# Last mLSTM head scanned alongside its projection, first output weights fetched inside the scan, and one weight pool and three product banks kept open behind it

## Chip, cores and metric

One core of one Trainium2 chip runs the whole program once. The metric is the device time of one execution in microseconds. The core has five engines: TensorE (PE, with its weight loads as PEld), VectorE (DVE), ScalarE (ACT), GpSimd (POOL) and SyncE (SP), which issues most of the transfers. TensorE writes its products into PSUM, eight banks of 128 x 512 float32; the other engines carry them on.

## What is computed

One layer of a diffusion backbone over 1152 rows (128 of context, block 0, and 1024 of latent tokens, blocks 1 to 8), width 1024. Two head groups run side by side, then one output projection merges them and a SwiGLU FFN follows:

```python
aq, ak, av, mq, mk, mv, mo, mg = split(h @ w_in)
attn_o = attention(aq, keys, vals)
hm, st_f, st_b = mlstm_bidir(...)          # 4 heads, chunks of 128, forward and backward
hm = rmsnorm(hm) * sigmoid(mo)
mix = concat([attn_o, hm]) @ w_out
x = x + g1 * mix
x = x + g2 * swiglu(rmsnorm(x) * (1 + sc2) + sh2)
```

A chunk b of an mLSTM head and one direction needs the state C at its edge: `num = (q k^T * D) v + inter * (q C)`, and `C_next = decay * C + k^T (w * v)`. The forward state goes from block 1 to 8, the backward state from 8 to 1.

## The kernel before

Float32 products are made from parts: an operand is split into a rounded high part and the rest (`whi`/`wlo`, `th`/`tl`), and three products (high x high, high x low, low x high) are summed in one bank. `load_piece` (L141) loads 512 KB of a weight into a `raw` tile, ScalarE casts it to the high part (L157), and VectorE subtracts to get the low part (`sub`, L137).

The order of the work on each engine is not written out by hand. The program is traced as generators that are woven at given rates, `hot(n)` raises the priority of what it encloses, `tc.issue_after` orders an instruction behind another of the same engine, and a planner that simulates the engines with estimated times makes each engine's fixed order from that. The engines then wait for one another at run time only.

The stages around the change:

- `head_project(h)` (L774) projects one mLSTM head: first the queries of three groups of 384 rows, then keys, values and output gate of the nine blocks, 0 to 8. After each block `evac` copies the results, transposes the keys (`kT`, L797 to L799), and `update` (L811) makes the block's k^T(wv) for both directions. The forward state is linked at once on VectorE (L824); the backward addend is copied by ScalarE (L828) and kept in `raws`.
- `head_mlstm(h)` (L857) scans one head. It begins with seven backward links on VectorE (L862). For each block, `weights(b)` makes q k^T and the decay matrix in one product bank (L875 to L878), ScalarE takes the exponential (`dt`, L881), VectorE multiplies (`sd`, L883). Then come the products with the two states (L898, scaled into `it`, L901), with the values (L905), their sum (`nu`, L908), the division, the gate and the rmsnorm (`rsqrt`, L121 to L134, twelve small VectorE operations), a GpSimd multiplication (L928) and the store to `hm_d` (L931, L933). The scan of head h is woven into the projection of head h + 1. The last head's scan stands alone: three blocks' `weights` are made ahead, the scan's own products use the two `wi` banks, and the norm is made for three blocks at a time.
- Beside that last scan run `attn_out_first` (L1281: the attention half of the output projection for blocks 0 to 2, both halves n of the columns, with `out_block`, L1179) and the last part of the adaLN modulation (`ada_rest`, strip products L364). They borrow tiles: weights in the `iraw` and `ipair` tiles, gates in `gta`, operands in `mxa`.
- Then the pools are closed: `hTp`, `gp`, `mlp` and the weight pool `wpi`, and the two PSUM pools `wi` (2 banks) and `mm` (3 banks). New ones are opened on the same memory: four `mm` banks, one `po` bank, a weight pool of 4 pairs and 2 `raw` tiles, and a pool `wl` with a fifth pair. A tile in a new pool waits for the tiles that lay at its place.
- `prefill` (L1188) makes the mLSTM half of the output projection for nine blocks: it loads rows of `hm_d` (L1198, L1200), transposes them (`mix`, L116), splits them (L1227, L137), multiplies with two pieces of `w_out` for each half (L1183 to L1185), adds gated to x (L1144, L1145), and for blocks 0 to 2 makes the second norm. Attention of the second group of blocks is woven in. After that the FFN fills TensorE to the end (L1389 to L1391, L1155 to L1157).

## Time and profile before

| | us |
|---|---|
| median of three runs | 1533.34 (1533.31 to 1536.2) |
| the profiled execution | 1535.49 |
| its span, first to last instruction | 1533.7 |
| TensorE busy | 1475.5 |
| VectorE busy | 1019.8 |
| ScalarE busy | 772.3 |
| GpSimd busy | 266.7 |

The span is what the trace covers; the execution lasts 1.8 us longer. All times in traces count from the first instruction. An arrow names what ended a wait. Consecutive matmuls overlap, so the time from one start to the next is what one costs, and not its own duration. The granted clock is the share of TensorE's full clock, 1.00 where nothing is held back.

### The profile page before, as it was taken

The page shows a single profiled execution, that of the slowest core. Times are in us where ns is not written, and L with a number is a line of the kernel's source. Part 1 is how long each engine was busy: PE and PEld are TensorE (multiplying, and loading weights), DVE is VectorE, ACT ScalarE, POOL GpSimd, SP SyncE. Part 2 cuts the span into 40 slices and gives each one's busy share as a digit, 9 for nine tenths or more (in the row PEclk, how much of TensorE's full clock was granted, in tenths as well). Part 3 has the DMA queues.
Part 4 walks back from the last instruction along what each step waited for, and adds up shares of the span by engine and source line. Part 5 has one row for each costly group of instructions (what it writes and reads, how often), then busy time and mean ns, then how long its engine had stood idle before and what let it go on. Part 6 is the DMA issues. An engine that isn't in the chain of part 4 may idle for free.

```text
span 1533.7 us, 23404 instructions
## 1 busy us (share of the span) xinstructions
PE 1475.5 (96%) x8539; PEld 1242.4 (81%) x8539; DVE 1019.8 (66%) x2025; ACT 772.3 (50%) x1429; POOL 266.7 (17%) x354
## 2 busy tenths in 40 slices
PE   6799999999988899999999999999999999999997
PEld 3545567677766689999898989989898989999996
DVE  4887655838657875877646587887856584554454
ACT  4765475847644554555333445656553443323333
POOL 0213423333434341010010101001010101101110
PEclk9899999999999999999999999999999999999999
DMA  9664323524365666979645457977854454544441
GB/s 362 193 204 156 92 70 42 119 52 72 79 207 166 161 161 179 214 167 193 165 119 156 138 169 230 190 175 171 187 134 145 139 163 154 158 134 137 140 145 56
DMA packets 387113, 233.77 MB, mean 152 GB/s; under 512 B 170102, under 2 KB 347462, under 8 KB 386998
## 3 DMA queue, kind: packets, MB, share of 16 engines
q1 hardware_dynamic: 385006, 228.69, 54.7%
q10 hardware_dynamic: 1864, 3.20, 1.1%
q8 instruction: 67, 1.10, 0.3%
q14 instruction: 48, 0.39, 0.1%
q0 software_dynamic: 128, 0.39, 0.1%
HBM read 182.21 MB, written 11.69 MB: 126 GB/s over the span
## 4 chain that ended last, share of the span: by engine, by line
PE 61%; DVE 3%; ACT 1%; issue 0%; DVEq 0%
PE mm L1390 12%; PE mm L1391 12%; PE mm L1389 12%; PE mm L1155 5%; PE mm L1156 5%; PE mm L1157 5%; PE S L1075 3%; PE po L1099 2%; PE po L1100 2%; PE mm L1183 1%; PE mm L1185 1%; PE mm L1184 1%; DVE fl L1378 1%; DVE wlo L137 1%; DVE t L1144 0%; DVE x L1145 0%
## 5 line engine op out<-in xcount | busy, mean ns | idle before, releaser
L157 ACT CAST whi<-raw 128x1024 fp32r<-128x1024 f32 (+1 forms) x216 | 221.8, 1027 | 386.8 <-PE mm L1390 143.9
L137 DVE TENSOR_TENSOR wlo<-raw,whi 128x1024 fp32r<-128x1024 f32 (+1 forms) x216 | 260.4, 1206 | 182.4 <-ACT whi L157 180.8
L1390 PE MATMUL mm<-aTl,whi 128*128 128x384 f32 x1056 | 355.9, 337 | 2.7 <-DVE aTl L137 2.7
L1391 PE MATMUL mm<-aTh,wlo 128*128 128x384 f32 x1056 | 354.3, 336 | 0.0
L1389 PE MATMUL mm<-aTh,whi 128*128 128x384 f32 x1056 | 353.1, 335 | 0.0
L137 POOL TENSOR_TENSOR hl<-tn,hl 128x384 fp32r<-128x384 f32 x66 | 83.8, 1270 | 847.4 <-ACT hl L1412 755.5
L1390 PEld LDWEIGHTS mm<-aTl,whi 128*128 128x128 f32 x1056 | 198.4, 188 | 3.9 <-DVE aTl L137 3.3
L1389 PEld LDWEIGHTS mm<-aTh,whi 128*128 128x128 f32 x1056 | 198.1, 188 | 0.5
L1391 PEld LDWEIGHTS mm<-aTh,wlo 128*128 128x128 f32 x1056 | 198.4, 188 | 0.1
L1156 PE MATMUL mm<-wlo,hl 128*128 128x512 f32 x372 | 145.5, 391 | 0.0
L1155 PE MATMUL mm<-whi,hl 128*128 128x512 f32 x372 | 144.2, 392 | 0.0
L1157 PE MATMUL mm<-whi,hl 128*128 128x512 f32 x372 | 142.8, 392 | 0.0
L1082 DVE SCALAR_TENSOR_TENSOR pl<-pr,st,ph 128x1152 f16<-128x1152 f32 (+1 forms) x72 | 96.3, 1337 | 36.6 <-ACT ph L1081 36.5
L1078 ACT ACTIVATE pr<-S,st 128x1152 f32<-128x1152 f32 (+1 forms) x72 | 81.3, 1129 | 38.4 <-DVE st L1077 36.6
L1077 DVE TENSOR_REDUCE st<-S 128x1 f32<-128x1152 f32 (+1 forms) x72 | 88.8, 1233 | 11.9 <-PE S L1075 11.3
L1081 ACT ACTIVATE ph<-pr,st 128x1152 f16<-128x1152 f32 (+1 forms) x72 | 83.8, 1164 | 22.7 <-DVE st L1080 9.9
L506 PE MATMUL wi<-headw,hT 128*128 128x384 f16 x288 | 93.9, 326 | 0.2 <-ACT th L792 0.2
L508 PE MATMUL wi<-headw,hT 128*128 128x384 f16 x288 | 93.9, 326 | 0.0
L507 PE MATMUL wi<-headw,hT 128*128 128x384 f16 x288 | 93.9, 326 | 0.0
L1075 PE MATMUL S<-kst,qT 128*128 128x384 f32 (+1 forms) x400 | 84.9, 344 | 4.0 <-ACT pr L1078 3.9
L1144 DVE TENSOR_TENSOR t<-mm,gl 128x512 f32<-128x512 f32 x102 | 68.7, 684 | 24.7 <-DMA gl<-g_d 9.3
L1157 PEld LDWEIGHTS mm<-whi,hl 128*128 128x128 f32 x372 | 69.9, 188 | 14.4
(396 smaller groups left out, 2639.8 us busy)
## 6 DMA issues: line engine op xcount, KB each, us to landing
raw<-in_w_gu_dram SPq DMA_DIRECT2D x132, 512.0 KB
raw<-in_w_down_dram SPq DMA_DIRECT2D x60, 512.0 KB
a<-in_w_ada_dram SPq DMA_DIRECT2D x24, 512.0 KB
gl<-g_d SPq DMA_DIRECT2D x36, 256.0 KB
aw<-in_w_ada_dram SPq DMA_DIRECT2D x16, 512.0 KB
iraw<-in_w_in_dram SPq DMA_DIRECT2D x32, 256.0 KB
raw<-in_w_out_dram SPq DMA_DIRECT2D x12, 512.0 KB
x<-in_x_sample_dram SPq DMA_DIRECT2D x11, 512.0 KB
```

The lines of the kernel that those rows point to most:

```text
L137: (dve if eng == "dve" else pool).tensor_tensor(out=out, in0=full, in1=hi, op=ALU.subtract)
L157: nc.scalar.copy(hi[:, :n], raw[:, :n])
L506: mm(ps[:, :n], ah, wh[:, k % 2, c0 : c0 + n], start=(k == 0), stop=False)
L507: mm(ps[:, :n], ah, wl[:, k % 2, c0 : c0 + n], start=False, stop=False)
L1075: mm(S[:, n, 0:w], qT[:, h, :], kst[kv][:, t, c0 + n * w : c0 + (n + 1) * w], start=(t == 0), stop=(t == 1))
L1082: dve.scalar_tensor_tensor(out=plv, in0=prv, scalar=st[:, 3:4], in1=phv, op0=ALU.mult, op1=ALU.subtract)
L1155: mm(ps, ah, wh[:, k % 2, :], start=(k == 0), stop=False)
L1156: mm(ps, ah, wl[:, k % 2, :], start=False, stop=False)
L1157: mm(ps, al, wh[:, k % 2, :], start=False, stop=(k == nk - 1))
L1389: mm(ps, wh[:, k, :], th[:, k, :], start=(k == 0), stop=False)
L1390: mm(ps, wh[:, k, :], tl[:, k, :], start=False, stop=False)
L1391: mm(ps, wl[:, k, :], th[:, k, :], start=False, stop=(k == KD - 1))
```

## The change

- **The last head's projection and scan.** Its blocks are projected in the order 0, 8, 7, ..., 1, and the backward state, not the forward one, is linked as they come. The forward links (seven) are issued in the scan, one for each block, by `link(0, b)`. The scan's generator is started inside the projection of the last block, so that `weights(0)` is issued there.
- **The end of head 2's scan.** Its rsqrt, multiplication and stores become a function `tail`, which is issued behind the `sd` of block 2 of the last scan. The weight pieces of `attn_out_first` are ordered behind `dt` and `sd` of that block too. The copy of the keys of block 1 has a raised priority.
- **First output weights.** A function `ahead` loads rows 0 and 1 of `hm_d` into the place of a query tile and the first two pieces of `w_out` of the prefill, one after the other, through a part of `gta`, before the old pools are closed.
- **Pools.** The weight pool stays open to the end. Its tiles carry new tags in twos, and five pairs are used in turn, two of them in new pools (`wq`, `wl`). The `mm` pool stays open with its three banks; a pool `mm1` adds one bank, which every fourth request of `bank()` takes. Queries of a head are one tile, not three.
- **`out_block`.** Four products with the weights' high parts, four with their low parts, and four with the input's low part come one after the other; before, the three stood together for each k.

The diff, cut to its core:

```diff
+DOWNWARD = [(0,)] + [(b,) for b in range(NB - 1, 0, -1)]
-    es_wp = ExitStack()
-    wp = es_wp.enter_context(tc.tile_pool(name="wpi", bufs=1, reuse_waits="tile"))
+    wp = ctx.enter_context(tc.tile_pool(name="wpi", bufs=1, reuse_waits="tile"))
+    turn_of = [0]
     def bank():
-        return psum["mm"].tile([P, 512], F32, name=nm("mm"), tag="mm")
+        turn_of[0] += 1
+        at = psum["mm"] if "mm1" not in psum or turn_of[0] % 4 else psum["mm1"]
+        return at.tile([P, 512], F32, name=nm("mm"), tag="mm")
...
-        raw = raw or wp.tile([P, 1024], F32, name=nm("raw"), tag="raw", bufs=2)
+        raw = wp.tile([P, 1024], F32, name=nm("raw"), tag="iraw1", bufs=2) if raw is None else raw
...
-            at, bufs = (wp, 4) if loaded["n"] else (wl, 1)
-            own = [at.tile([P, 1024], F32R, name=nm(t), tag=t, bufs=bufs) for t in ("whi", "wlo")]
+            tag = ("wl", "ipair1", "ipair0", "iraw0", "wq")[loaded["n"]]
+            at = homes.get(tag, wp)
+            own = [at.tile([P, 1024], F32R, name=nm(t), tag=tag, bufs=2) for t in ("whi", "wlo")]
...
     def head_project(h, st):
+        along = 1 if h == NH - 1 else 0
...
-            st["act"] = nc.scalar.copy(kT, pt[:, 0:P])
+            with hot(300 if b == 1 and along else 0):
+                st["act"] = nc.scalar.copy(kT, pt[:, 0:P])
...
-                if d == 0 and b > 0:
-                    st["dve"] = dve.scalar_tensor_tensor(out=cn, in0=states[0, b], scalar=decb[:, b * 4 + h : b * 4 + h + 1], in1=add,
+                if d == along and b > 0:
+                    col = d * 64 + b * 4 + h
+                    st["dve"] = dve.scalar_tensor_tensor(out=cn, in0=states[d, b], scalar=decb[:, col : col + 1], in1=add,
                                              op0=ALU.mult, op1=ALU.add)
-                    states[0, b + 1] = cn
+                    states[d, b + 1 - 2 * d] = cn
...
-        for i, _ in enumerate(linear_tok(pieces, P, 3 * P, evac, SINGLES)):
+        for i, _ in enumerate(linear_tok(pieces, P, 3 * P, evac, DOWNWARD if along else SINGLES)):
...
+            if along and i == (NB - 1) * KD:
+                next(st["scan"])
...
     def head_mlstm(h, st):
+        def link(d, b):
+            col = d * 64 + b * 4 + h
+            dve.scalar_tensor_tensor(out=st["raw"][b], in0=states[d, b], scalar=decb[:, col : col + 1], in1=st["raw"][b],
+                                     op0=ALU.mult, op1=ALU.add)
+            states[d, b + 1 - 2 * d] = st["raw"][b]
+        alone = h == NH - 1
+        if not alone:
+            for b in range(NBL, 1, -1):
+                link(1, b)
...
-        ahead = [weights(b) for b in range(depth)]
+        ahead = []
+        if alone:
+            ahead.append(weights(0))
+            yield
+        ahead += [weights(b) for b in range(len(ahead), depth)]
+        while alone and tails:
+            with behind("sd"):
+                tails.pop()()
         yield
         for b in range(NB):
+            if alone and 1 <= b < NBL:
+                link(0, b)
...
     def out_block(ws, n, th, tl):
         for k in range(4):
-            wh, wl = ws[n][k // 2]
+            wh = ws[n][k // 2][0]
             mm(ps, th[:, k], wh[:, k % 2, :], start=(k == 0), stop=False)
-            mm(ps, th[:, k], wl[:, k % 2, :], start=False, stop=False)
-            loaded["pe"] = mm(ps, tl[:, k], wh[:, k % 2, :], start=False, stop=(k == 3)).ins
+        for k in range(4):
+            mm(ps, th[:, k], ws[n][k // 2][1][:, k % 2, :], start=False, stop=False)
+        for k in range(4):
+            loaded["pe"] = mm(ps, tl[:, k], ws[n][k // 2][0][:, k % 2, :], start=False, stop=(k == 3)).ins
...
-        hms = [load_hm(0), load_hm(1)]
-        ws = [out_pieces(1, 0)]
+        hms = hms_first
+        ws = [ws_first]
...
-                    with tc.issue_after(sts[-1]["act"].ins), tc.issue_after(sts[-1]["dve"].ins):
+                    with tc.issue_after(sts[-1]["act"].ins), tc.issue_after(sts[-1]["dve"].ins), behind("dt"), behind("sd"):
...
+        spare = gt[:, 0:2].rearrange("p a b -> p (a b)")
+        def ahead():
+            rows = mlp.tile([P, NCH * CT], F32, name="hmra", tag="qTm", bufs=2)
+            hms = [rows[:, b * 512 : (b + 1) * 512] for b in range(2)]
+            for b in range(2):
+                dma(hms[b], hm_d[0][b * P : (b + 1) * P, :])
+            return out_pieces(1, 0, spare), hms
...
     emit(scan)
+    ws_first, hms_first = ahead()
     es1.close()
-    es_wp.close()
     es_d.close()
-    for name, bufs in (("mm", 4), ("po", 1)):
+    for name, bufs in (("mm1", 1), ("po", 1)):
...
-    wp = ctx.enter_context(tc.tile_pool(name="wp", bufs=1, reuse_waits="tile"))
+    homes["wq"] = ctx.enter_context(tc.tile_pool(name="wq", bufs=1, reuse_waits="tile"))
-    wl = ctx.enter_context(tc.tile_pool(name="wl", bufs=1, reuse_waits="tile"))
+    homes["wl"] = ctx.enter_context(tc.tile_pool(name="wl", bufs=1, reuse_waits="tile"))
```

68 lines of the change are left out of this document (37 added, 31 removed).

## The prediction

> **What bounds the kernel now.** I read the page's busy shares first, then the busy time by stage, then TensorE's waits inside the stages that are not full, and last the single instructions around those waits.
>
> ```profile
> span 1533.7 us, 23404 instructions
> ...
> PE 1475.5 (96%) x8539; PEld 1242.4 (81%) x8539; DVE 1019.8 (66%) x2025; ACT 772.3 (50%) x1429; POOL 266.7 (17%) x354
> ```
>
> TensorE is busy 1475.5 of 1533.7 us, so it bounds the kernel, and an edit that leaves its work alone can win at most what it idles or runs at a low clock. The table of stages says where that is (columns: width, then busy us of PE, PEld, DVE, ACT, POOL, then the granted clock, DMA share, GB/s).
>
> ```profile
> 0.00:140.00 140.00, 114.32 (x770) 64.44 (x770) 104.53 (x364) 84.12 (x175) 21.38 (x25) 0.95 0.72 241
> 437.00:442.00 5.00, 4.68 (x38) 3.83 (x35) 2.73 (x10) 2.80 (x11) 1.42 (x5) 1.00 0.96 353
> 442.00:448.00 6.00, 3.20 (x23) 2.38 (x22) 5.68 (x15) 5.34 (x14) 2.65 (x4) 1.00 0.54 200
> 448.00:455.00 7.00, 6.19 (x32) 4.11 (x32) 5.91 (x18) 1.53 (x6) 2.62 (x2) 0.51 0.69 224
> 455.00:482.00 27.00, 27.00 (x173) 19.98 (x172) 17.35 (x47) 11.29 (x35) 11.27 (x12) 1.00 0.35 112
> 482.00:493.00 11.00, 7.49 (x38) 4.67 (x37) 10.56 (x39) 7.44 (x22) 5.62 (x7) 1.00 0.87 282
> 493.00:502.00 9.00, 8.04 (x36) 6.04 (x37) 6.71 (x18) 3.16 (x4) 1.70 (x4) 1.00 0.73 234
> 502.00:510.00 8.00, 6.29 (x33) 5.17 (x32) 5.71 (x8) 3.63 (x5) 4.37 (x4) 1.00 1.00 326
> 510.00:519.00 9.00, 5.86 (x29) 4.85 (x28) 8.49 (x25) 4.49 (x9) 4.32 (x3) 1.00 0.61 145
> 519.00:524.00 5.00, 4.80 (x19) 3.96 (x18) 4.69 (x14) 5.00 (x9) 0.00 (x0) 0.66 0.31 57
> 560.00:1500.00 940.00, 937.19 (x5146) 868.27 (x5145) 622.24 (x885) 422.74 (x553) 86.69 (x68) 1.00 0.61 163
> ```
>
> The start (0 to 140) is not touched, and from 560 on 937.19 of 940 us are busy. The scan of the last head begins at 442, the prefill of the output projection at about 487; between 442 and 524 TensorE idles 2.80 + 0.81 + 3.51 + 0.96 + 1.71 + 3.14 + 0.20 = 13.1 us (width less busy time). Twice the clock falls as well: 0.51 over 448 to 455, of which 6.19 us were busy, loses 6.19 x 0.49 = 3.0 us of work; 0.66 over 519 to 524 loses 4.80 x 0.34 = 1.6. So **17.7 us** is all there is to win here.
>
> ```profile
> PE S L1075 <- ACT pr L1078: 3.1, 1, 3.1
> PE mm L875 <- DVE sd L883: 2.1, 1, 2.1
> PE mm L1184 <- DVE wlo L137: 1.9, 4, 0.6
> PE mm L1185 <- DVE mx L137: 1.7, 1, 1.7
> PE mm L1183 <- ACT mx L1227: 1.1, 1, 1.1
> PE wi L905 <- DVE nu L908: 0.8, 2, 0.4
> PE mm L364 <- DVE sd L883: 0.8, 1, 0.8
> PE mm L875 <- ACT kT L799: 0.6, 1, 0.6
> ```
>
> These eight waits, all between 437 and 524, are 12.1 us of it, and VectorE is behind most of them.
>
> **The change part by part.** It adds and removes no matmul, no decay link, no weight cast and no transfer; it moves them. So I cost positions and take TensorE's work as constant.
>
> *Start of the last scan.* Now, seven backward links (L862), the whole rsqrt of the previous head and two weight subtractions stand on VectorE before or between the first `sd` (L883), and the three product banks stay held until `sd` has read them.
>
> ```profile
> 446.85 0.49 PE L875 MATMUL mm<-qT,kT 128*128 128x128 f32 x2 [2.13 <-DVE sd L883]
> ```
> ```profile
> 446.38 0.41 DVE L883 TENSOR_TENSOR sd<-mm,dt 128x256 f32<-128x256 f32 x1
> ...
> 451.13 2.09 DVE L862 SCALAR_TENSOR_TENSOR cs<-cs,decb,cs 128x129 f32<-128x129 f32 x1
> ...
> 489.01 1.23 DVE L137 TENSOR_TENSOR wlo<-raw,whi 128x1024 fp32r<-128x1024 f32 x1
> ```
> ```profile
> L862 DVE SCALAR_TENSOR_TENSOR cs<-cs,decb,cs 128x129 f32<-128x129 f32 x6 | 3.8, 634 | 0.0
> ```
>
> Afterwards weights(0) with its `sd` lies in the projection of block 1 (where TensorE is full: 4.68 of 5.00), the seven links (3.8 us for six of them) go to the blocks of the scan, forward ones now, since the backward ones take the forward ones' place in the projection, and the subtractions and the rsqrt are queued behind the third `sd`. At 442 `sd`(0) is there; weights(1), weights(2), one pair of L905 and the first strip products then fill TensorE while ScalarE and VectorE make `sd`(1) and `sd`(2). What is late next is block 1's keys (kT, 0.6 us now) and the first `dt`/`sd` pair. Of the 2.80 + 0.81 = 3.61 us idle I keep 1.2 (0.6 for kT, as much for `sd`): gain **2.4**, bounds 0 and 3.6. Queued behind the waiting subtractions on VectorE are only the first product's operands; their cover is the scan itself, and without it one subtraction costs 1.23.
>
> *The clock.* The dip starts right after these gaps. With 1.2 us idle I expect none, because 482 to 493 idles 3.51 in 11 us and keeps 1.00: gain **3.0**, bounds 0 and 3.0. By the Trainium skill ("TensorE: Matmul & The Clock Gate", The HAM clock gate) one idle window of about 3.4 us halves the clock and one busy window restores it. The trace agrees with the half; by that rule a dip that stays would cost an estimated 1.7 and leave this term 1.3.
>
> *End of the scan and the first output weights.*
>
> ```profile
> 476.66 0.37 SPq L931 DMA_DIRECT2D hm_d<-hm  x1
> 480.84 0.82 SPq L1198 DMA_DIRECT2D hmr<-hm_d  x2
> 481.75 0.90 SPq L156 DMA_DIRECT2D raw<-in_w_out_dram  x2
> ```
> ```profile
> 487.24 1.09 PE L116 MATMUL mm<-ident,hmr 128*128 128x128 f32 x8 [0.59 <-DVE nu L908]
> 489.42 0.50 PE L1183 MATMUL mm<-whi,mx 128*128 128x512 f32 x1 [1.09 <-ACT mx L1227]
> ```
> ```profile
> 466.56 0.69 DVE L1322 TENSOR_TENSOR gta<-mm,gta 128x512 f32<-128x512 f32 x1 [0.58 <-PE mm L1185]
> ```
>
> Now the rows of h and the weights are asked for only at 480.84 and 481.75, and the transposes wait for a scan bank (`nu`). Afterwards four transfers move ahead on SP: two rows of h and two weight pieces of 512 KB. The first piece needs the gates of half 0, last read at 466.56 + 0.69 = 467.3; the second needs the same staging tile after the first's subtraction. From issue to the end of its subtraction a piece takes 8.5 us now (481.75 to 489.01 + 1.23), so they would be ready by about 476 and 484, or 4 earlier with the earlier scan: the weights leave the path. What is late next is the h rows: the store at 476.66 waits for block 2's scaling, and its landing for the load; on SP nothing urgent stands behind them but the next strip's weights, whose cover is the scan. If block 2 comes some 4 us earlier, the h rows land before the scan ends, the transposes take a product bank instead of a scan bank, and their chain (2.2 us from 487.24 to 489.42) runs under the last scan blocks. Of 3.51 I keep 1.0 (the two `nu` waits and a rest): gain **2.5**, bounds 0 and 3.5. The 0.96 of 493 to 502 are two waits for a low part whose piece was loaded late; its staging tiles are now free when the first half ends: gain **0.9**, bounds 0 and 1.0.
>
> *Lower parts last.*
>
> ```profile
> 508.98 0.39 PE L1183 MATMUL mm<-whi,mx 128*128 128x512 f32 x1
> 509.21 0.40 PE L1184 MATMUL mm<-wlo,mx 128*128 128x512 f32 x1
> ```
>
> The same twelve matmuls; the first use of the input's low part moves from third to ninth place. At 0.23 us from start to start that is 6 x 0.23 = 1.4 us more for VectorE, out of the 1.71 idle in 502 to 510: gain **1.4**, bounds 0 and 1.7. The weight load per matmul is unchanged (8539 of each).
>
> *Banks.* Four interchangeable banks become three and one that every fourth request must take. I put it at nothing because the FFN is full, and keep the other end below.
>
> *Links beside GpSimd.* The link of 2.09 us ran beside this instruction and ended with it, against 0.34 for the others ((3.8 - 2.09) / 5).
>
> ```profile
> 450.84 2.23 POOL L928 TENSOR_TENSOR hm<-hm,ry 128x1152 f32<-128x1152 f32 x1 [4.67 <-DVE dn L915]
> ```
>
> GpSimd is busy 11.27 of 27 us in the scan (42%). Seven links moved there, each held up to 1.75 longer, cost VectorE 7 x 0.42 x 1.75 = 5.1 at most, with 27 - 17.35 = 9.65 us free; each link is issued a block before its state is read. I charge **1.2** between 0 and 5.1, nearer the free time. The Trainium skill ("SBUF — State Buffer", Who interferes with whom) says that a VectorE instruction with two SBUF inputs and a GpSimd one reading SBUF lock each other out for a whole instruction. The trace agrees (2.09 beside 2.23), and the rule speaks against this part of the change.
>
> *Left alone.* The 3.14 at 510 to 519 (S waits for the softmax's exponential) and the 1.6 of clock after it: VectorE is busy 8.49 of 9 there with other work; I take 0, between a loss of 3 and a gain of 4.7.
>
> **Sum:** 2.4 + 3.0 + 2.5 + 0.9 + 1.4 - 1.2 = 9.0 us. The profiled execution took 1535.49 us (span 1533.7 and 1.8 around it), which would become 1526.5; it stands 2.15 above the median of the runs, 1533.34, from which I count: 1533.34 - 9.0 = **1524.3**.
>
> **The rivals.** *Links in the way:* the 5.1 falls on TensorE in full instead of 1.2: 1524.3 + 3.9 = **1528.2**. For it speaks the 2.09; against it, the block of lead. *Nothing gained:* the planner issues the early loads and links where they stood, or the gap only moves from `sd` to the h rows; the time stays at about **1533**. For it: order here is a plan by estimated times, not by these. *The fourth bank (slower):* requests of raised priority, six of attention and eighteen of the second norm, take the turn of a bank whose holder is issued later, and TensorE waits one evacuation each.
>
> ```profile
> L1144 DVE TENSOR_TENSOR t<-mm,gl 128x512 f32<-128x512 f32 x102 | 68.7, 684 | 24.7 <-DMA gl<-g_d 9.3
> ```
>
> 24 x 0.684 = 16.4 us against a gain of 9.0: **1540.7**, deciding from 9.0 / 24 = 0.38 us each. Against it: 5146 matmuls in 937 us are 0.18 each, a product of 24 takes 4.4 us, and a bank comes round only after three others. *More:* the stall at 514 and its clock go too: 1524.3 - 4.7 = **1519.6**.
>
> **How the numbers follow.** Forecast 0.54 (its own range 1520.5 to 1528), links 0.14, nothing gained 0.13, the fourth bank 0.13, more 0.06. A measurement of this kernel tells about 0.2% (3.1 us) from no change, so faster means below 1530.3 and slower above 1536.4: faster 0.72 (forecast, more, nearly all of links), same 0.15, slower 0.13. The range is 1517 to 1534: below it 0.03, above it the bank and some of "nothing gained", 0.16.
>
> **What would show it.** Right: TensorE at least 85% busy in the first 6 us after the projection, clock 1.00 there, no wait on `wlo`, `mx` low or `nu` over 0.5, output matmuls beginning about 7 us earlier. Wrong: a clock of 0.5 after the projection, waits of L898 on a link, or waits on banks spread through the FFN. The forecast fails if the plan around the attention of the second group changes for the worse by over 3 us.

## The result and the profile after

In ten runs of each, the kernel after took 1531.24 us (median, 1527.66 to 1535.33) and the kernel before 1535.99 (1533.31 to 1538.19). The ratio is 0.9971, 95% interval 0.9962 to 0.9979: **4.5 us faster** (0.0029 x 1536; the medians differ by 4.75), where 9.0 were forecast. The predicted 1524.3 lies 6.9 below the measured time; 2.65 of that is the base, since before's median was 1533.34 in the three runs I counted from. The direction was right and the size was not. The time lies in the range, but the prediction's own line for "faster", 1530.3, was drawn from the lower base: by it 1531.24 would have counted as the same, while the ratio is clear of 1. The profiled execution of the kernel after took 1531.07 us.

From the page of the kernel after:

```profile
span 1529.3 us, 23410 instructions
...
PE 1473.0 (96%) x8539; PEld 1244.7 (81%) x8539; DVE 1015.8 (66%) x2025; ACT 770.4 (50%) x1429; POOL 268.8 (18%) x354
```

TensorE's busy time is 2.5 us less (1475.5 before), yet its idle time fell only from 58.2 to 56.3 us (span less busy). The idle time was mostly moved, not removed. The table by stage (columns as in the prediction) shows where to:

```profile
442.00:448.00 6.00, 4.29 (x37) 3.76 (x35) 4.60 (x14) 4.94 (x17) 2.74 (x4) 1.00 0.01 3
448.00:455.00 7.00, 5.89 (x51) 4.14 (x52) 6.97 (x31) 4.80 (x16) 0.46 (x1) 1.00 0.70 225
455.00:482.00 27.00, 24.21 (x149) 17.48 (x148) 21.38 (x60) 12.49 (x36) 13.78 (x14) 1.00 0.59 188
482.00:493.00 11.00, 9.11 (x51) 6.80 (x50) 9.27 (x19) 5.34 (x12) 5.03 (x4) 1.00 0.84 257
493.00:502.00 9.00, 7.39 (x36) 6.08 (x36) 5.87 (x19) 3.51 (x9) 1.88 (x3) 1.00 0.58 189
502.00:510.00 8.00, 8.00 (x40) 6.78 (x39) 7.51 (x11) 3.39 (x5) 7.15 (x4) 1.00 1.07 268
510.00:519.00 9.00, 7.06 (x35) 5.48 (x34) 8.68 (x34) 6.72 (x12) 3.84 (x3) 0.95 0.64 137
519.00:524.00 5.00, 4.42 (x12) 3.28 (x11) 3.58 (x17) 4.61 (x9) 0.79 (x1) 0.50 0.38 99
...
560.00:1500.00 940.00, 936.74 (x5141) 870.62 (x5140) 620.69 (x881) 420.12 (x552) 88.63 (x68) 1.00 0.61 162
```

Read width less PE busy. The first two rows idle 1.71 + 1.11 = 2.8 us (before 3.6) and the clock is 1.00 where it was 0.51. But 455 to 482, full before, now idles 2.8. The next four rows idle 1.9, 1.6, 0.0 and 1.9 (before 3.5, 1.0, 1.7, 3.1). The clock at 519 to 524 still falls, to 0.50. From 560 on nothing changed (936.74, before 937.19). The waits of TensorE between 430 and 560 name the new idle time (us in total, times, longest):

```profile
PE mm L120 <- ACT y L1414: 1.8, 1, 1.8
PE mm L1219 <- ACT mx L1265: 1.8, 1, 1.8
PE mm L370 <- DVE sd L903: 1.8, 1, 1.8
PE mm L1219 <- DVE mx L141: 1.6, 1, 1.6
PE mm L370 <- DMA ip<-in_w_ada_dram: 1.5, 2, 0.8
PE mm L479 <- ACT hmx L470: 0.9, 1, 0.9
PE mm L1221 <- DVE ir L141: 0.7, 1, 0.7
PE wi L936 <- DVE nu L939: 0.6, 2, 0.4
```

The waits on S, on `kT` and on `wlo` are gone; the one on `sd` is 1.8 instead of 2.1 + 0.8. The two on `mx` stay (1.8 + 1.6, before 1.1 + 1.7); the 1.6 now stands before a block's first product (L1219), which reads the high part. The wait on `y` (in the second norm) is new, and so are those on `hmx`, `ir` and `ip`, in the middle of the scan.

Of the signs that the prediction named, the clock of 1.00 after the projection came. TensorE was busy 4.29 of the first 6 us there (71%, where 85% were named), a wait of 1.6 ended with the subtraction for `mx` (at most 0.5 was named), and the output matmuls began only 0.8 us earlier than before (489.42), not 7:

```profile
488.60 1.19 PE L1219 MATMUL mm<-whi,mx 128*128 128x512 f32 x4 [1.81 <-ACT mx L1265]
```

None of its signs of being wrong showed either: what went wrong is not among them.

**The two executions by work done.** To see gains and losses by stage I weighed each matmul with the usual start-to-start distance of its shape in the trace (the 35th percentile) and read, for a time of before, when the other execution had done the same sum. The table has the change of that offset in us in each stretch (minus is a gain). All rows are against the one profiled execution of before; the first column, in which the work of all kernels is the same, is chance of the execution (−0.4 to +3.1). Runs of one kernel spread over some 3 to 10 us, so whether a kernel is faster is read from the ratios below, and only the place of a gain from this table.

| kernel | to 150 | 150–442 | 442–454 (start of scan) | 454–478 (middle) | 478–544 (end, prefill) | 544 to end | sum |
|---|---|---|---|---|---|---|---|
| after | 0.6 | 0.8 | −4.6 | +4.1 | −5.5 | 0.3 | −4.4 |
| after again (a0) | 0.6 | 0.4 | −4.6 | +5.2 | −5.7 | −1.0 | −5.1 |
| before, other bank split (e8) | 1.7 | 0.6 | −1.4 | −0.2 | −2.5 | 0.2 | −1.7 |
| before, new order of products (e11) | 0.0 | 0.3 | −1.6 | 0.6 | 0.2 | 1.0 | 0.5 |
| after, start of scan undone (e10) | 0.8 | 1.7 | −4.0 | +6.2 | −2.5 | −0.9 | 1.3 |
| after, links in one piece (e4) | 1.2 | 0.2 | −4.6 | +3.8 | −5.6 | −1.0 | −6.1 |
| after, links spread (e5) | 2.0 | 0.3 | −5.5 | +4.7 | −5.6 | 2.0 | −1.9 |
| after, no early rows and weights (e6) | 1.2 | 0.4 | −3.8 | +3.2 | −3.4 | −1.6 | −4.1 |
| after, old order of products (e7) | 2.4 | 0.1 | −4.6 | +4.0 | −3.5 | −0.2 | −1.8 |
| after, both of these (e14) | 1.5 | 0.4 | −4.6 | +2.4 | −3.1 | 0.9 | −2.6 |
| after, tail in its old place (e1) | 1.6 | 0.5 | −3.2 | +1.1 | −3.9 | −1.9 | −5.7 |
| after, two tiles exchanged (e2) | 3.1 | 0.4 | −4.6 | +2.1 | −4.2 | 0.8 | −2.5 |
| after, weights not behind the third `sd` (e12) | 0.5 | 2.4 | −2.3 | +3.1 | −7.1 | 0.9 | −2.6 |
| after, banks in other order (e3) | 1.3 | −0.4 | −4.6 | +4.4 | −7.5 | 0.5 | −6.2 |
| after, e2 and e3 together (e9) | −0.4 | −1.0 | −4.6 | +3.6 | −4.2 | 0.0 | −6.6 |
| e9, strip's weights first (e13) | −0.2 | −1.0 | −4.6 | +1.5 | −4.1 | −1.8 | −10.2 |

So the theory to test: the start of the scan and its end gained about what was forecast, the middle gave 4 back because the moved transfers and subtractions now stand in its way, and the order of the banks cost 1. Rivals: the links are the cause at one of these places; the early loads or the order of products are the whole gain; the fourth bank costs.

### The profile page after: what moved, and what is told of

Same layout as the page of the kernel before. It is cut to its first block, busy times and chain, and to the rows that moved or that the text cites. A ratio compares the mean times of both kernels' runs of the same rounds, so it can differ in the third digit from the quotient of the medians.

```text
span 1529.3 us, 23410 instructions
## 1 busy us (share of the span) xinstructions
PE 1473.0 (96%) x8539; PEld 1244.7 (81%) x8539; DVE 1015.8 (66%) x2025; ACT 770.4 (50%) x1429; POOL 268.8 (18%) x354
## 4 chain that ended last, share of the span: by engine, by line
PE 78%; DVE 5%; DMA 3%; ACT 3%; issue 1%; POOL 1%; SPq 0%; ACTq 0%; DVEq 0%; POOLq 0%
PE mm L1437 11%; PE mm L1436 11%; PE mm L1435 11%; PE mm L1191 5%; PE mm L1192 5%; PE mm L1193 5%; PE S L1111 4%; PE wi L514 3%; PE wi L513 3%; PE wi L512 3%; PE mm L1219 2%; PE po L1136 2%; PE po L1135 2%; PE mm L1221 2%; PE mm L1223 2%
## 5 line engine op out<-in xcount | busy, mean ns | idle before, releaser
L163 ACT CAST whi<-raw 128x1024 fp32r<-128x1024 f32 x214 | 219.2, 1026 | 367.8 <-PE mm L1436 146.9
L141 DVE TENSOR_TENSOR wlo<-raw,whi 128x1024 fp32r<-128x1024 f32 x214 | 257.7, 1204 | 170.5 <-ACT whi L163 167.0
```

The costliest lines, as they stand in the source:

```text
L141: (dve if eng == "dve" else pool).tensor_tensor(out=out, in0=full, in1=hi, op=ALU.subtract)
L163: nc.scalar.copy(hi[:, :n], raw[:, :n])
```

## The experiments

Every kernel was timed in five rounds, with 5 to 12 runs of each. The ratios are against the kernel before in the same group of runs; its medians in the four groups, each on another chip, were 1535.59, 1535.84, 1535.49 and 1535.97.

### The same kernel again: a0_after

No edit. Expected:

> The changed kernel again, unaltered, as the mark for the runs beside it. Its lead over the kernel before should be 4 to 5 us again (ratio 0.9971). If the lead moves by over 2 us, single differences of 1 us between the other kernels say nothing.

Measured: 1531.92 us, ratio 0.9969 [0.9956, 0.9982]. The gain repeats.

### Do the links matter? e4_links_first and e5_links_late

The prediction had the links spread over the scan. The trace of the kernel after shows that they are not (VectorE, start and duration):

```profile
444.86 0.35 DVE L878 SCALAR_TENSOR_TENSOR cs<-c,decb,cs 128x129 f32<-128x129 f32 x1
...
447.60 0.41 DVE L903 TENSOR_TENSOR sd<-mm,dt 128x256 f32<-128x256 f32 x1
...
450.05 0.36 DVE L878 SCALAR_TENSOR_TENSOR cs<-cs,decb,cs 128x129 f32<-128x129 f32 x1
```

The first and the last of the seven are shown: all run within 5.6 us at the start, around the second `sd`. e4 issues them there in one piece:

```diff
+        if alone:
+            for b in range(1, NBL):
+                link(0, b)
...
-            if alone and 1 <= b < NBL:
-                link(0, b)
```

> The changed kernel with the seven forward links issued together at the start of the last scan, where the backward ones stood before. Theory of the prediction (the links' place clogs VectorE and so costs the clock): TensorE idles over 3 us in the first 8 us after the projection, the clock falls to 0.5, and the kernel is 4 to 5 us slower than the changed one. Rival (in the changed kernel the links ran between 444.9 and 450.4 anyway, and what kept the clock is weights(0) being ready with its sd inside the projection): within 1.5 us of the changed kernel, clock 1.00 after the projection.

Measured: 1530.14 us, 0.9963 [0.9948, 0.9978], as the rival has it; the clock stays up:

```profile
448.00:455.00 7.00, 6.44 (x53) 4.62 (x54) 6.97 (x31) 4.81 (x16) 0.46 (x1) 1.00 0.74 222
```

e5 really spreads them, each behind the `sd` of the next block:

```diff
-            if alone and 1 <= b < NBL:
-                link(0, b)
...
+            if alone and 1 <= b < NBL:
+                with tc.issue_after(st["sd", min(b + 1, NB - 1)]):
+                    link(0, b)
```

> The kernel after with each forward link tied behind the sd of the block after it, so that the seven links really are spread over the scan; in the kernel after they ran in one row at its start (444.9 to 450.4) beside the second and third sd. Theory (the links at the start are why 1.8 us of the wait on sd stay): that wait shrinks by about 1 us, ratio 0.9965. Rival (sd waits for the chain from product over exponentials to VectorE, links or no links): the wait stays at 1.5 to 2, the time within 0.7 us of the kernel after, ratio 0.997.

Measured: 1534.61 us, 0.9990 [0.9980, 1.0001], slower than the kernel after. Three of TensorE's waits between 430 and 560, in the same columns:

```profile
PE wi L931 <- ACT it L934: 1.7, 1, 1.7
...
PE wi L931 <- DVE cs L878: 1.1, 1, 1.1
PE mm L370 <- DVE sd L903: 0.7, 1, 0.7
```

The wait on `sd` fell to 0.7 as the theory has it, so the links are 1 us of it. But that won nothing: the strip's matmul behind it began at 448.09, against 448.06 in the kernel after, and a scan block then waited 1.1 for a state (`cs`) and another 1.7. The rest of the lost time stands after 544 (+2.0 in that stretch: TensorE waited 2.63 us at 581 for the attention's transposed exponentials). No cause for that one is shown. What follows: the place of the links explains neither the gain nor its missing half.

### Is the early start the gain? e10_no_early

```diff
-            if along and i == (NB - 1) * KD:
-                next(st["scan"])
```

> The kernel after, but the last scan isn't begun inside the last head's projection: its first weights (product, exponentials, sd) are issued at the end of the projection with the second and third, as before. The other parts stay. Theory (this part took the first clock dip away, since the place of the links did not): sd(0) comes back to about 446, TensorE idles over 3.5 us between 442 and 455, the granted clock falls to about 0.5 there again, and 2 to 4 us of the gain go: ratio about 0.999. Rival (the dip went because the rsqrt and the store of the head before were put off, or because of a small change of phase): clock 1.00 at 442 to 455, within 1 us of the kernel after, ratio 0.997.

Measured: 1537.31 us, 1.0010 [0.9998, 1.0022]. The size was more than the theory gave: without the early `weights(0)` nothing is left of the gain, 0.0039 x 1536 = 6.0 us. But its mechanism was wrong. The clock by stage:

```profile
448.00:455.00 7.00, 6.44 (x50) 5.21 (x51) 6.67 (x27) 4.03 (x11) 0.00 (x0) 1.00 0.46 146
455.00:482.00 27.00, 22.30 (x146) 15.84 (x145) 22.06 (x61) 12.27 (x38) 12.14 (x12) 0.94 0.56 187
...
493.00:502.00 9.00, 7.22 (x26) 5.84 (x27) 5.50 (x14) 4.19 (x12) 0.52 (x2) 0.63 0.79 240
```

At 448 to 455 it is 1.00; the idle time of 442 to 455 is 1.81 + 0.56 = 2.4, less than in the kernel after, and the start of the scan gains 4.0 of the 4.6. So the early `weights(0)` is not what keeps the clock up there. The loss comes later: 4.7 us idle in the 27, and a clock of 0.63 at 493. One gap makes most of it, here on TensorE:

```profile
465.69 1.23 PE L934 MATMUL wi<-va,sd 128*128 128x129 f32 x4 [3.69 <-DVE nu L937]
```

and on VectorE, whose `nu` it waits for:

```profile
458.64 2.06 DVE L944 TENSOR_TENSOR dn<-dn,QT 128x2 f32<-128x2 f32 x1
...
464.04 1.25 DVE L135 TENSOR_TENSOR rt<-ry 128x3 f32<-128x3 f32 x1
465.22 0.41 DVE L937 TENSOR_TENSOR nu<-wi,it 128x258 f32<-128x258 f32 x1
```

with GpSimd beside them:

```profile
458.56 2.12 POOL L958 TENSOR_TENSOR hm<-hm,ry 128x1152 f32<-128x1152 f32 x1 [0.93 <-DVE ry L137]
...
464.02 1.26 POOL L1359 TENSOR_TENSOR x1a<-x1a,gta 128x512 f32<-128x512 f32 x1 [1.34 <-DVE ry L137]
```

The usual time of that `dn` (L944) is in its own view, min, median and max in ns:

```profile
L944 DVE TENSOR_TENSOR dn<-dn,QT x36: 142/163/2057, 224.6 to 496.8; 128x2 f32<-128x2 f32 x36
```

Its 163 ns became 2057. It ended with GpSimd's scaling of the nine blocks of head 2 (458.56 + 2.12 = 460.68, 458.64 + 2.06 = 460.70); an `rt` took 1.25 beside GpSimd's 1.26. The first stands in the chain from numerator to output, the second straight ahead of `nu`. My reading, which no run separates: without the early start the put-off closing work of head 2 meets the scan where it has no lead. A kernel with neither the early start nor the put-off work, but with the rest of the change, was not run.

### Early loads and the order of products: e6_no_ahead, e7_old_k, e14_start_alone, e11_new_k

e6 loads rows and first weights where they were loaded before:

```diff
-        hms = hms_first
-        ws = [ws_first]
+        hms = [load_hm(0), load_hm(1)]
+        ws = [out_pieces(1, 0)]
...
-    ws_first, hms_first = ahead()
```

> The changed kernel with the first two rows of h and the first two output weight pieces asked for in the prefill again, as before the change. Theory (the early fetch is worth 3 us at the end of the scan): waits of the output matmuls on wlo or on the rows of h come back between 482 and 500, together 2 to 4 us, and the kernel is 2 to 4 us slower than the changed one. Rival (what starts the prefill is the gates tile gta and the rows of h, which are no earlier): within 1 us.

e7 takes the products of `out_block` back into their old order:

```diff
-            wh = ws[n][k // 2][0]
+            wh, wl = ws[n][k // 2]
             mm(ps, th[:, k], wh[:, k % 2, :], start=(k == 0), stop=False)
-        for k in range(4):
-            mm(ps, th[:, k], ws[n][k // 2][1][:, k % 2, :], start=False, stop=False)
-        for k in range(4):
-            loaded["pe"] = mm(ps, tl[:, k], ws[n][k // 2][0][:, k % 2, :], start=False, stop=(k == 3)).ins
+            mm(ps, th[:, k], wl[:, k % 2, :], start=False, stop=False)
+            loaded["pe"] = mm(ps, tl[:, k], wh[:, k % 2, :], start=False, stop=(k == 3)).ins
```

> The changed kernel with the three products of each k side by side again in the output blocks. Theory (a late low part is hidden by eight matmuls instead of two): 1 to 2 us slower than the changed kernel, with waits on wlo or on the low part of mx of 0.3 to 1.7 us each in the prefill. Rival (the first high part is late as well, so that the order does not matter): within 0.7 us.

e14 is both edits, which leaves the start of the scan, what is put off behind it, and the pools:

> The kernel after with the interleaved order of the output matmuls and without the early h rows and first weights, so that only the early start of the last scan, what is put off behind it, and the banks and pools are left of the change. Theory (the parts pay only together: the start hands 4.6 us to the middle of the scan, which gives 4 of them back unless the later waits are gone as well): ratio 0.9985 to 1.000. Rival (the start is the whole gain and the other parts are worth nothing): ratio as in the kernel after, 0.997.

e11 is the kernel before with the same lines the other way round, so with the new `out_block` alone:

> The kernel before with one part of the change alone: the twelve matmuls of an output block go through all high parts first, then the weights' low parts, then the input's low parts. Theory (undoing it cost 2 to 3 us, so it is worth as much alone): the waits on the input's low part (1.7) and half of those on wlo (1.9) go, TensorE idles 2 to 3 us less between 493 and 519, ratio about 0.9985. Rival (it is worth something only where the first output weights come early, as in the changed kernel): the wait turns to wlo and the time stays within 1 us of before, ratio 0.9995 to 1.0005.

Measured: e6 1531.48 us, 0.9972 [0.9962, 0.9983]; e7 1534.03, 0.9989 [0.9979, 0.9999]; e14 1533.02, 0.9978 [0.9968, 0.9988]; e11 1537.32, 1.0011 [1.0001, 1.0021]. In e6 the rows of h do come late, and TensorE waits for them:

```profile
PE mm L120 <- DMA hmr<-hm_d: 2.7, 1, 2.7
```

Yet the time is that of the kernel after: what the early rows save is spent on the first input tile (`mx` 1.8 at 488.60) and in the middle of the scan (3.8 to 5.2 lost with them in after, a0, e4 and e7, 3.2 and 2.4 without, in e6 and e14). The new order of products made the kernel before no faster, if anything slower (e11: the wait on S was 4.1 there). Undoing it in the kernel after cost 0.0018 x 1536 = 2.8 us, more than its theory's 1 to 2, with intervals that touch, but undoing it together with the early loads cost only 0.0007 x 1536 = 1.1, with intervals that overlap. So I read both parts together as **about 1 us, not surely above nothing**, where the prediction had 4.8, and leave open how they divide. The two traces say where it went: both parts gain 2.4 at the end (5.5 against e14's 3.1), and the middle loses 1.7 more with them (4.1 against 2.4). e14 lies between its two expectations, about as far from one as from the other; by its median the early start, what is put off behind it and the pools are 0.0022 x 1536 = 3.4 us, most of the gain.

### What the middle gave back: e1_tail_back, e2_swap_homes, e12_no_behind

In the kernel after, `hmx`, the strip's rows, lies in a tile that still holds head 2's output, whose put-off store is issued late. On ScalarE:

```profile
463.62 0.58 ACT L470 COPY hmx<-mm 128x512 f32<-128x512 f32 x1 [2.00 <-DMA hm_d<-hm]
```

and on SyncE, which issues the transfers:

```profile
457.87 0.37 SPq L963 DMA_DIRECT2D hm_d<-hm  x1
...
463.60 0.27 SPq L477 DMA_DIRECT2D hmx<-in_b_ada_dram  x1
...
466.10 1.02 SPq L1369 DMA_DIRECT2D hmra<-hm_d  x2
...
469.74 0.93 SPq L451 DMA_DIRECT2D ip<-in_w_ada_dram  x2
```

The store goes at 457.87 (453.10 before); ScalarE's copy into `hmx` waits 2.00 for it, and SyncE stands until 463.60. The strip's last weights (L451) are asked for at 469.74, behind the early rows (L1369), though the kernel is ahead of before, which asked at 468.42. e1 puts the closing work of head 2 back:

```diff
-                if h != NH - 2:
-                    tails.pop()()
+                tails.pop()()
```

> The kernel after, but the closing part of head 2 (rsqrt, scaling, store) is issued at the end of head 2's scan again, not behind the third sd of the last scan. Theory (the put-off store holds the strip rows hmx, and that is about half of what the middle of the scan gave back): the wait on hmx (0.9) and ScalarE's 2.0 behind the store go, TensorE idles under 2 of the 27 us in 455 to 482 instead of 2.8, and the clock at 442 to 455 stays 1.00; the kernel is 0 to 2 us faster than the one after, ratio 0.996 to 0.997. Rival (the put-off is what keeps the start of the scan free): the wait on sd at 448 grows from 1.8 to over 2.5, the clock there falls below 0.9, and the kernel is 2 us slower, ratio 0.9985.

e2 exchanges `hmx` with the early rows' tile:

```diff
-        hmx = mlp.tile([P, NB, P], F32, name="hmx", tag="hm", bufs=2).rearrange("p b n -> p (b n)")
+        hmx = mlp.tile([P, NCH * CT], F32, name="hmx", tag="qTm", bufs=2)
...
-            rows = mlp.tile([P, NCH * CT], F32, name="hmra", tag="qTm", bufs=2)
+            rows = mlp.tile([P, NB, P], F32, name="hmra", tag="hm", bufs=2).rearrange("p b n -> p (b n)")
```

> The kernel after with two tiles exchanged: the strip rows hmx lie where the early h rows (hmra) lay and the other way round, so that hmx no longer waits for the put-off store of head 2. Theory (that store holds hmx, which costs the mid-scan 0.9 to 2 us): the wait of 0.9 on hmx at 464 and ScalarE's 2.0 on the store go, TensorE's idle time in 455 to 482 falls from 2.8 to under 1.9, and the time falls by 1 to 2 us: ratio about 0.996. Rival (another wait stands right behind it): idle time of 455 to 502 together as in the kernel after (6.3 us), the time within 0.7 us of it, ratio 0.997.

e12 drops the order that keeps the strip's output weights behind the third `sd`:

```diff
-                    with tc.issue_after(sts[-1]["act"].ins), tc.issue_after(sts[-1]["dve"].ins), behind("dt"), behind("sd"):
+                    with tc.issue_after(sts[-1]["act"].ins), tc.issue_after(sts[-1]["dve"].ins):
```

> The kernel after without the order that puts the strip's first output weights (load, cast, subtraction) behind the third block's exponentials and sd; the load now goes as early as its staging tile allows, as before. Theory (that order delays the low parts ir, so it is the other half of what the middle of the scan gave back): the waits on ir (0.7) and on the next strip weights (0.8) shrink, idle time in 455 to 482 falls from 2.8 to about 1.5, and sd at the start waits up to 1.2 us longer, so the time is within 1 us of the kernel after, ratio 0.997. Rival (the order is what keeps the clock up at the start): two subtractions of 1.23 stand before the second sd again, its wait is over 2.5, the clock at 448 to 455 falls to 0.8 or less and the kernel is 2 to 3 us slower, ratio 0.9985.

Measured: e1 1529.62 us, 0.9958 [0.9946, 0.9969]; e2 1529.64, 0.9962 [0.9949, 0.9975]; e12 1534.18, 0.9987 [0.9974, 1.0000]. The stages of e1:

```profile
448.00:455.00 7.00, 5.40 (x41) 3.71 (x41) 7.00 (x19) 4.07 (x10) 2.11 (x1) 0.76 0.54 161
455.00:482.00 27.00, 26.67 (x162) 19.79 (x163) 22.54 (x69) 14.32 (x42) 11.49 (x12) 1.00 0.64 203
```

The middle is full again (0.3 idle, and 1.1 lost instead of 4.1), so in the trace the put-off closing work is what emptied it. The price is at the start, as the rival has it: the wait on `sd` is 2.4, and the clock 0.76 over 5.40 us, 1.3, which the kernel after doesn't pay. The time is the theory's: 0.0013 x 1536 = 2.0 us below the kernel after, with intervals that overlap. So putting this work off is not shown to pay. e2 tells the store's part alone. The idle time of 455 to 482 falls to 1.5:

```profile
455.00:482.00 27.00, 25.52 (x157) 18.25 (x154) 22.34 (x72) 13.67 (x40) 10.73 (x13) 1.00 0.65 208
```

and that of 455 to 502 to 1.48 + 1.50 + 1.06 = 4.0, from 6.3: the theory, for the trace. By time its interval and the kernel after's overlap. e12 shows the other side, the theory of the change itself:

```profile
448.00:455.00 7.00, 4.48 (x33) 3.48 (x34) 6.77 (x25) 4.21 (x16) 2.33 (x2) 0.82 0.68 224
```

2.5 us idle and a clock of 0.82 come back there (2.3 gained at the start instead of 4.6), nearly as the rival in that expectation said. By time the order is worth 0.0016 x 1536 = 2.5 us, with intervals that overlap a little; but the trace of e12 gets the loss back in the middle and at the end, and over 442 to 544 it is level with the kernel after (−6.3 and −6.0).

### The banks: e3_banks and e8_before_bank4

Because the product banks stay open, their pool is now opened ahead of the two scan banks (the line `for name, bufs in (("wi", 2), ("mm", 3))` became `(("mm", 3), ("wi", 2))`), which so come to lie on the banks of the last q blocks. On TensorE, the first product of the second head in the kernel after:

```profile
158.18 0.32 PE L849 MATMUL wi<-hT,headw 128*128 128x384 f16 x1 [2.14 <-ACT qraw L754]
```

and in e3, which opens the first two pools in the other order as well:

```profile
156.39 0.32 PE L848 MATMUL wi<-hT,headw 128*128 128x384 f16 x1
```

```diff
+    es_a = ExitStack()
+    pA = es_a.enter_context(tc.tile_pool(name="pA", bufs=4, space=PSUM, reuse_waits="tile"))
     es_b = ExitStack()
...
-    es_a = ExitStack()
-    pA = es_a.enter_context(tc.tile_pool(name="pA", bufs=4, space=PSUM, reuse_waits="tile"))
...
-    es_a.close()
     es_b.close()
+    es_a.close()
```

> The kernel after with the first two groups of banks opened in the other order, so that the two scan banks, which now come second, lie on banks of the product group again and not on the ones that hold the last q blocks. Theory: the wait of 2.1 at 156 to 158 (a scan bank's first product on the evacuation of q) goes, and the kernel is 0.8 us faster from 180 on, ratio about 0.9965. Rival: the wait only moves to the product banks, and the progress at 430 is the same as in the kernel after.

Measured: 1529.33 us, 0.9961 [0.9948, 0.9975]. The wait of 2.14 is gone, and 150 to 442 has −0.4 instead of +0.8: 1.2 us. The three kernels with this repair (e3, e9, e13) have −0.4 to −1.0 there, the eleven others with the change +0.1 to +2.4. By time the intervals of e3 and the kernel after overlap. e8 gives the kernel before the split of its banks into three and one:

```diff
+        turn_of[0] += 1
+        at = psum["mm"] if "mm1" not in psum or turn_of[0] % 4 else psum["mm1"]
...
-    for name, bufs in (("mm", 4), ("po", 1)):
+    for name, bufs in (("mm", 3), ("mm1", 1), ("po", 1)):
```

> The kernel before with its four product banks of the second half split into three and one that every fourth request takes, as the change has them. Theory (a bank comes round only after three others are evacuated): no difference, ratio 0.9995 to 1.0005, and the busy share of TensorE from 560 to 1500 stays within 1 us of 937.2. Rival (the prediction's slower case): 0.38 us or more lost at each of the 24 requests of raised priority, 9 us or more, ratio 1.006 or above.

Measured: 1535.88 us, 1.0000 [0.9990, 1.0011]: the theory. Since nothing else differs from the kernel before, this trace is also a second look at it:

```profile
448.00:455.00 7.00, 5.65 (x38) 3.92 (x39) 7.00 (x22) 2.47 (x10) 2.32 (x2) 0.76 0.65 175
...
560.00:1500.00 940.00, 937.07 (x5141) 868.74 (x5141) 620.62 (x884) 422.12 (x553) 87.78 (x68) 1.00 0.62 163
```

and two of its waits:

```profile
PE mm L1187 <- DVE rh L132: 2.9, 1, 2.9
...
PE S L1079 <- ACT pr L1082: 0.4, 1, 0.4
```

The clock dip at the start was 0.76 over 5.65 us, 1.4 of work and not 3.0. The wait on S was 0.4 and not 3.1, but its time did not go: a wait of 2.9, ended by VectorE's `rh` (of an rsqrt), followed within 4 us, and from 510 to 524 TensorE was busy 8.43 + 2.11 = 10.54 us, against 5.86 + 4.80 = 10.66 in the trace of before:

```profile
510.00:519.00 9.00, 8.43 (x39) 6.70 (x38) 8.90 (x29) 4.48 (x8) 3.74 (x2) 1.00 0.61 146
519.00:524.00 5.00, 2.11 (x15) 1.62 (x14) 5.00 (x12) 5.00 (x10) 1.27 (x1) 1.00 0.39 78
```

The waits on the low parts were smaller as well: `wlo` 1.0 instead of 1.9, `mx` 0.5 instead of 1.7. The trace of e11, which leaves the start of the scan as it was too, says the same of the clock, 0.79 over 6.96 us, 1.5:

```profile
448.00:455.00 7.00, 6.96 (x45) 4.98 (x43) 6.12 (x18) 1.95 (x7) 2.69 (x2) 0.79 0.71 225
```

So the dip differs from one execution to the next: up to 470 us before, e8 and e11 run the same instructions in the same order on every engine. The low parts may differ by the bank split, which lies in their stretch in e8.

### Both repairs, and the queue of SyncE: e9_banks_homes and e13_strip_first

e9 is e2 and e3 together:

> The kernel after with both repairs, the first two bank groups opened in the other order and the two tiles hmx and hmra exchanged. Theory (both losses are separate: 1.2 us at 156 to 190, and about 2 us of hmx in the middle of the scan): faster than the kernel after by 2 to 3 us, ratio 0.995 to 0.9955. Rival (what is gained in the middle of the scan is lost again at its end, where the input tile of the second half waits for gta): no faster than with the banks alone, ratio 0.996 to 0.9965.

Measured: **1527.01 us, 0.9944 [0.9932, 0.9956]**, 8.6 us faster than before, the fastest kernel here; its interval lies below that of the kernel after. Its trace shows the banks (−1.0 instead of +0.8), but hardly the exchange: the middle loses 3.6 instead of 4.1, and the end gains 4.2 instead of 5.5. In the middle another wait took the place of the one on `hmx` (TensorE):

```profile
PE mm L369 <- DMA ip<-in_w_ada_dram: 2.7, 3, 1.4
```

e13 is e9 with the early rows and weights behind the strip's last load:

```diff
-            dma(a4, w_ada[...])
+            loaded["ada"] = dma(a4, w_ada[...]).ins
...
+            with behind("ada"):
                 for b in range(2):
                     dma(hms[b], hm_d[0][b * P : (b + 1) * P, :])
                 return out_pieces(1, 0, spare), hms
```

> The kernel with both repairs (bank groups in the other order, hmx and hmra exchanged), and the early rows of h and first weight pieces tied behind the last load of the strip's own weights, which they stood ahead of on SyncE. In the kernel with both repairs the strip's last weights are asked for at 466.1, behind the h rows that wait for a store, and TensorE waits 2.7 in all for such weights. Theory (this queue order is the rest of what the middle of the scan gives back): the waits on the strip's weights fall below 1.5, idle time in 455 to 482 from 2.7 to under 1.7, and the ratio goes from 0.9944 to 0.9935 to 0.994. Rival (the middle of the scan is bound by chains of several engines, and something else is late next, or the h rows come too late for the transposes): idle time of 455 to 502 together as before the edit (6 us), ratio 0.994 to 0.9955.

Measured: 1529.30 us, 0.9961 [0.9947, 0.9976]. The queue was the cause of that wait, but not of the time:

```profile
PE wi L935 <- DVE sd L902: 2.2, 1, 2.2
...
PE mm L369 <- DMA ip<-in_w_ada_dram: 0.5, 1, 0.5
```

`ip` fell from 2.7 to 0.5 and the middle lost only 1.5, but a scan block at 483 then waited 2.2 for its `sd`; 455 to 502 idle 1.67 + 2.29 + 1.61 = 5.6, against 6.0 in e9. By time it lies above both expectations, and its interval overlaps that of e9: no gain is shown.

## Where the prediction was right and where it failed, step by step

- **Start of the scan: right in place, smaller in size, wrong in two reasons.** The trace gained 4.6 where 2.4 + 3.0 = 5.4 were forecast. Measured from the two other traces with the start of before, e8 and e11, it gained 3.2 and 3.0. Of the causes named, the rsqrt and the subtractions put off behind the third `sd` are shown in the trace: with either back in its place the gap at the start is 2.3 to 2.4, the clock dips and the stretch gains only 3.2 (e1) or 2.3 (e12). By time the order of the subtractions is worth up to 2.5 us (e12), and putting the rsqrt off is not shown to pay (e1). The links played no part (e4, e5). The early `weights(0)` is needed, all of the gain goes without it (e10), but not for the start: without it the scan meets a gap of 3.69 at 465.
- **The clock: mis-sized.** I took 3.0 from the one profiled execution. The same start showed a dip worth 1.4 in e8 and 1.5 in e11. The dip has no fixed price; about 2, the mean of the three, was the better term. The Trainium skill ("TensorE: Matmul & The Clock Gate", The HAM clock gate) says that the activity window runs freely, and that the same kernel meets it in another phase at its start from run to run. The traces are in line with it in the middle of a kernel: the clock was 0.51, 0.76 and 0.79 over 448 to 455 in three executions with the same start. The two gaps ahead of the dip were alike in all three, 0.6 to 0.7 and 2.1 us. That the phase is the reason no run shows.
- **"Their cover is the scan": the step that failed.** The prediction let four transfers, the closing work of head 2 and two subtractions move behind or into the scan at no cost, and so counted the gains at its start and at its end in full. The scan had been the one full stretch, 27.00 of 27; once its start came 4.6 earlier, what feeds it came no earlier, and the middle gave back 4.1. In the traces, the put-off closing work with the store that holds `hmx` (e1, e2) and the early rows ahead of the strip's weights on SyncE (e13) are part of it. But added up over 442 to 544 the kernel after gains 6.0 and, again, 5.1, and the kernels with a repair of the middle lie around that: 6.0 (e1), 6.7 (e2), 6.3 (e12), 5.2 (e9), 7.2 (e13). Repairing one wait brought the next one forward, so I read this part as bound by several chains and not by one wait; which of them would have to go together is open.
- **End of the scan, `wlo` and lower parts: the terms that this emptied.** The trace gained 5.5 where 2.5 + 0.9 + 1.4 = 4.8 were forecast, but 3.1 of that is there without the two parts (e14), and the middle pays 1.7 for the rest: by time they are worth about 1 us. So by time most of what is missing lies in these terms, 1.1 for 4.8; e14 has 3.4 for the start and the pools, where the start and the links were put at 5.4 - 1.2 = 4.2. e8, which has neither part, is itself 2.5 ahead of the trace of before in that stretch. The waits on `wlo` went; those on `mx` stayed (1.8 and 1.6). The second can't be one for the low part, since it stands before a first product; my reading, which no run tests, is that a product bank is late there. And the output matmuls began 0.8 us earlier and not 7.
- **The banks.** At nothing for the fourth bank: right (e8). But the order in which the pools are opened was not looked at, and it cost 1.2 us by the trace, 284 us ahead of the last scan (e3).
- **Links beside GpSimd, 1.2: not seen.** In the kernel after, the links at 444.86 and 450.05 took 0.35 and 0.36. The lock itself is real (e10), but there it struck `dn` and `rt`.
- **Left alone, at 0: about right.** From 510 to 524 TensorE idles 2.5 us instead of 3.3; the wait on S gave way to others, the one on `y` first, and the clock dip at 519 stayed (0.50).

Together, from the trace: −4.6 + 4.1 − 5.5 + 0.8 at the banks, and 0.6 + 0.3 outside: −4.3, against −4.4 in the spans. What stays open: how the last 1 us divides between early loads and order of products, and the 2 us at 581 in e5.

## What to carry to other kernels

A stall that is taken away ahead of a full stretch is kept only if what feeds that stretch gets earlier too: before giving a moved transfer the cover of a full stage, ask whether the stage stays full once the change has worked. Put-off work keeps its buffers: look up who takes the tile next (here exchanging two tiles and opening two pools in another order about doubled the gain, from 0.9971 to 0.9944; the trace shows the part of the pools). And a stall or clock dip read from one execution has no fixed size: the dip at the start of the scan was worth 3.0, 1.4 and 1.5 in three executions with the same work there, so a forecast should take less than all of it. Nor is a wait that is gone a gain yet: S waited 3.1 in one trace and 0.4 in another, and the stretch around it was equally busy (10.66 and 10.54 of 14 us).

## What the hardware showed unexpectedly

- A VectorE instruction on two numbers a partition took 2.06 us instead of 0.16 beside a GpSimd instruction of 2.12 that had begun 0.08 earlier, and both ended within 0.02 us (e10). The Trainium skill ("SBUF — State Buffer", Who interferes with whom) has this lock: the engine that issues first keeps the shared ports for the whole instruction, and the other is blocked. The trace agrees with it. What it adds is the price: a short instruction of a chain loses almost the whole length of the other, 1.9 us here.
- A clock of 0.51 to 0.82 at 448 to 455 stood behind single gaps of 2.1 to 2.4 us on TensorE (before, e8, e11, e1, e12); with a longest gap of 1.8 or less it was 1.00 in eleven executions, and 0.76 in one, e6. The sum of the idle time over 442 to 455 tells less: 2.8 in the kernel after at 1.00, 0.97 + 1.60 = 2.6 in e1 at 0.76. This holds for that place alone: at 482 to 493 the clock was 0.84 in e2 with a longest gap of 1.24 us, and from 510 to 524 it was 1.00 in e3 with one of 1.8.
